# Packing small matmuls into groups of the PE array in an eight-core decoder kernel: gates in row and column groups, pooling bands of 144 columns, sample states in pairs

## The chip, the cores and the metric

The kernel runs on all 8 cores of one Trainium2 chip (two dies: cores 0 to 3 and 4 to 7). Each core computes its own prompt and its own samples. The metric is the device time of the slowest core, in microseconds (us); it is 1 to 2 us longer than the longest span in the trace of the same execution. Some executions fall in a slower state in which one die runs at a lower granted clock (the share of the full TensorE clock that the throttle lets through); only fast executions are compared here. Because the slowest of eight counts, I often give two numbers: the time of the slowest core, and the mean of the spans of all eight cores in the same fast executions. The second is usually less noisy. In the profiles PE is the matmul engine (TensorE), DVE VectorE, ACT ScalarE, POOL GpSimd and SP SyncE; a PSUM bank is one of the buffers into which the PE writes.

## The reference

One layer of a hybrid decoder. Only the parts that the change touches are kept:

```python
D_MODEL, SEQ, DEC_SEQ = 1024, 2048, 4      # per core: one prompt of 2048 rows, 16 samples of 4 rows
GLA_HEADS, GLA_DK, GLA_DV, GLA_GATE_RANK = 4, 128, 256, 16

def token_mix(xn, s0, buf, pos0, p):
    q, k, v, gz, og, u, ga, gb = jnp.split(xn @ p['w_in'], split_points(), axis=-1)     # gz: 16 columns
    log_a = log_sigmoid(gz @ p['w_gk_up'] + p['b_gk']) / 16                             # decay logits
    o, s_new = gla_chunked(q, k, v, log_a, s0)     # S = exp(b_end) * S + k_dec^T v   per head (128 x 256)
    ...

def pool_mix(u, buf, pos0, w_mix, scale):          # trailing means over windows 2, 4, 8, 16 by channel group
    win = hi - cs_shifted_by_w
    d = win / cnt - u
    y = einsum('btgc,gcd->btgd', d, w_mix) * scale
```

After that come a cross-attention over 256 memory tokens and a channel mixer of 4096 hidden units. They make up most of the time and are not changed.

## The kernel before

The kernel declares operations with their reads, their writes and an estimated cost. A list scheduler of its own then fixes one order per engine, from a model of the costs. The engines run their orders strictly one after the other. A DMA is tied to the PE operation that lies `ahead` = 30 us of *declared* PE cost before it, and PSUM banks are given out in the modelled order.

```python
def op(self, eng, fn, reads=(), writes=(), cost=0.1, dma=False, ..., ahead=None, after=()):
    if eng == "pe":
        self.peclk += cost                       # clock of declared PE cost
        self.pelog.append((self.peclk, i))
    ...
    if ahead is not None:                        # a DMA may start once this PE operation is done
        k = bisect.bisect_right(self.pelog, (self.peclk - ahead, 1 << 60)) - 1
        if k >= 0:
            deps[self.pelog[k][1]] = 0
```

Low-rank gate input and decay logits of a tile of 1024 rows (there are two tiles). The output has 16 rows in the first and the contraction is 16 deep in the second, so most of the 128 x 128 array is empty:

```python
def gzp():
    for hf in range(2):
        b = self.bank()
        self.mm(self.pb[b][:16, :], [(self.wgz[:, kc, :], A[:, kc, hf * 512:(hf + 1) * 512]) for kc in range(8)])
        self.cp("act", self.gzT[:, hf * 512:(hf + 1) * 512], self.pb[b][:16, :])
def decay():
    for h in range(4):
        for hf in range(2):
            b = self.bank()
            self.mm(self.pb[b][:, :], [(self.wgk[:, h * 128:(h + 1) * 128], self.gzT[:, hf * 512:(hf + 1) * 512])])
            self.act(T1[:, h, ...], self.pb[b][:, :], AF.Exp, scale=-1.0, bias=self.ncols[:, h:h + 1])
        ...
```

Sample states. The 64 sample rows (16 samples of 4) are the partitions of `kdts` and `vts`. A mask column keeps one sample's 4 rows, so that a 128-deep matmul gives that sample's outer product. Each state (512 KB in fp32) is loaded, copied to bf16, updated in place and stored:

```python
for i in range(SB):                              # SB = 16
    sf = self.ring("s0f", self.s0f); sb_ = self.ring("s0b", self.s0b); kb = self.ring("kblk", self.kblk)
    self.dma("sp", sf[...], I["sgla"][i], nb=1.4)
    self.cp("act", sb_[:, :, :], sf[:, :, :])
    self.ts("dve", kb[:, :], self.kdts[:, :], self.bmk[:, i:i + 1], ALU.mult, also=[sf[:, :, :]])
    self.mmx([... old state times q of sample i, 8 matmuls of 4 columns ...])
    for hp in range(2):
        b = self.bank()
        self.mms([(self.pb[b][:, (h % 2) * 256:(h % 2 + 1) * 256],
                   [(kb[:, h * 128:(h + 1) * 128], self.vts[:, h * 256:(h + 1) * 256])]) for h in (2 * hp, 2 * hp + 1)])
        for h in (2 * hp, 2 * hp + 1):
            self.stt("dve", sf[:, h, :], sf[:, h, :], self.eBs[:, h, i:i + 1], self.pb[b][...], ALU.mult, ALU.add)
        if hp == 0:
            yield                                # other work may come in between
    self.dma("sp", O["sgs"][i], sf[...], nb=1.4)
    yield
```

The 1 MB load of the pooling mix weights, declared without a word about the loads of x:

```python
def precompute(self):
    self.dma("sp", self.pmf[:, :], I["wpmT"][:, :])
```

## Time and profile before

The median of the first six runs was 1296.51 us (1294.37 to 1332.79). The page of the slowest core (core 4) says first how busy each engine was, and the third line gives the engines' shares of the chain of work that ended last.

```profile
span 1293.1 us, 23059 instructions; the slowest of 8 cores (1283.4 to 1293.1 us)
...
PE 1251.0 (97%) x8342; PEld 645.2 (50%) x8490; DVE 654.8 (51%) x1088; ACT 651.4 (50%) x1333; POOL 67.8 (5%) x131
...
PE 91%; DMA 5%; issue 2%; DVE 1%; ACT 1%; DVEq 0%; POOL 0%; ACTq 0%; SPq 0%; POOLq 0%
```

The PE does nearly everything that counts: 97% busy and 91% of the chain. The table of two stretches of core 4 shows where it is not busy. Its first line names the columns.

```profile
core 4: us, PE busy (x) PEld busy (x) DVE busy (x) ACT busy (x) POOL busy (x), PEclk, DMA share, GB/s
0.00:40.00 40.00, 24.59 (x316) 17.12 (x319) 14.27 (x23) 15.80 (x37) 5.37 (x14) 0.81 0.90 197
...
350.00:400.00 50.00, 49.69 (x353) 27.00 (x359) 30.49 (x72) 41.60 (x88) 0.53 (x1) 1.00 0.47 134
```

In the first 40 us the PE works for 24.6 us and the DMA engines are 90% busy: this is the load of x and of the first weights. From 350 to 400 us, where the sample states run, the PE is hardly ever free.

The next lines are from the timeline of core 4 (start, length, engine, line, output and inputs, shape, count, and in brackets the idle time before with what ended it). Ends of matmuls are modelled, so one reads the distance from one start to the next.

```profile
23.25 1.01 PE L842 MATMUL pb<-ident,xn_101 128*128 128x128 bf16 x8 [4.25 <-DVE xn_101 L877]
...
38.57 1.01 PE L842 MATMUL pb<-ident,xn_102 128*128 128x128 bf16 x8 [3.74 <-DVE xn_102 L877]
...
46.69 1.89 PE L814 MATMUL pb<-actT,wgz 128*16 128x512 bf16 x8
...
343.45 1.06 ACT L861 ACTIVATE s0b_140<-s0f_119 128x1024 bf16<-128x1024 f32 x1 [1.05 <-DMA s0f_119<-sgla]
...
371.69 0.34 PE L833 MATMUL pb<-qs,s0b_140 128*128 128x4 bf16 x8
371.90 0.38 PE L824 MATMUL pb<-vts,kblk_142 128*128 128x256 bf16 x2
372.12 0.61 PE L842 MATMUL pb<-ident,xn_102 128*128 128x128 bf16 x8
...
684.15 3.62 PE L814 MATMUL pb<-actT,wgz 128*16 128x512 bf16 x16
```

The two waits at the top are for normalised rows of x, and so for their loads. One group of 16 gate matmuls takes 3.46 us (16 pitches of 216 ns). Two outer products of one sample, a "visit" to the states, take 0.22 us, from 371.90 to 372.12. Last, the issues of the sync engine's DMA queue on the same core: the fourth and the last load of x, then the mix weights.

```profile
17.09 0.33 SPq L915 DMA_DIRECT2D xst_90<-xp  x1
...
26.52 0.33 SPq L915 DMA_DIRECT2D xst_94<-xp  x1
...
31.00 0.33 SPq L915 DMA_DIRECT2D pmf<-wpmT  x1
```

### The profile page before, as it was taken

What the parts mean: (1) busy time and instruction counts of PE and PEld (TensorE: products, weight loads), DVE (VectorE), ACT (ScalarE), POOL (GpSimd) and SP (SyncE); (2) the same over time, 40 slices, a digit from 0 to 9 for tenths busy, and PEclk for the clock granted to TensorE, in tenths of its full rate; (3) what the DMA queues carried; (4) which work ended last, traced back from release to release, by engine and by line L of the source; (5) the groups of instructions that cost most, each with busy time, mean ns of one, the idle gap of its engine ahead of it and who ended that gap; (6) DMA issues with size and microseconds to landing.
All of it is one profiled execution on the core that took longest, in us unless ns stands there. A gap on an engine that the chain in (4) does not pass through costs nothing.

```text
span 1293.1 us, 23059 instructions; the slowest of 8 cores (1283.4 to 1293.1 us)
## 1 busy us (share of the span) xinstructions
PE 1251.0 (97%) x8342; PEld 645.2 (50%) x8490; DVE 654.8 (51%) x1088; ACT 651.4 (50%) x1333; POOL 67.8 (5%) x131
## 2 busy tenths in 40 slices
PE   6899999999999999999999999999999999999997
PEld 4444556444455544444544455644455544454453
DVE  3564755231458765444675356623244754444446
ACT  3555966556587742132236278755558753120304
POOL 1100000000000000000000010100100000000000
PEclk7999999999999999999999999999999999999999
DMA  8979369243829569686779585858862333342503
GB/s 180 187 161 180 70 129 188 42 99 75 219 91 222 138 167 169 113 155 137 154 171 191 93 150 109 147 102 145 142 185 38 62 66 66 66 77 54 98 2 139
DMA packets 33675, 160.93 MB, mean 124 GB/s; under 512 B 4598, under 2 KB 5246, under 8 KB 22156
## 3 DMA queue, kind: packets, MB, share of 16 engines
q0 software_dynamic: 18112, 104.29, 47.9%
q1 hardware_dynamic: 15452, 55.15, 12.3%
q8 instruction: 70, 1.15, 0.4%
q14 instruction: 41, 0.34, 0.1%
HBM read 241.63 MB, written 22.80 MB: 204 GB/s over the span
## 4 chain that ended last, share of the span: by engine, by line
PE 91%; DMA 5%; issue 2%; DVE 1%; ACT 1%; DVEq 0%; POOL 0%; ACTq 0%; SPq 0%; POOLq 0%
PE pb L814 81%; PE pb L824 6%; PE pb L842 3%; DMA wt_45<-wu 1%; PE pb L833 1%; DMA xst_93<-xp 1%; DMA s0f_121<-sgla 1%; DMA xst_89<-xp 1%; DMA sgs<-s0f_121 0%; DMA xst_91<-xp 0%; DVE S L882 0%; DVE xn_102 L882 0%; ACT xn_102 L861 0%; DVE xh L882 0%; DVE xn_101 L882 0%
## 5 line engine op out<-in xcount | busy, mean ns | idle before, releaser
L882 DVE SCALAR_TENSOR_TENSOR xh<-pb,r_178,xh 128x512 f32<-128x512 f32 x128 | 95.7, 750 | 90.8 <-PE pb L814 90.6
L814 PE MATMUL pb<-actT,wt_45 128*128 128x512 bf16 x436 | 100.5, 379 | 0.7
L814 PE MATMUL pb<-actT,wt_44 128*128 128x512 bf16 x435 | 99.1, 379 | 0.7
L861 ACT ACTIVATE tmp_98<-pb 128x512 f32<-128x512 f32 (+1 forms) x48 | 28.4, 591 | 111.7 <-PE pb L814 109.3
L814 PE MATMUL pb<-actT,wt_43 128*128 128x512 bf16 x313 | 71.8, 379 | 0.4
L814 PE MATMUL pb<-actT,wtG 128*128 128x512 bf16 x309 | 71.6, 379 | 0.6
L814 PEld LDWEIGHTS pb<-actT,wt_45 128*128 128x128 bf16 x448 | 43.0, 98 | 50.5 <-issue 0.4
L871 DVE TENSOR_TENSOR xh<-pb,xh 128x512 f32<-128x512 f32 x64 | 44.2, 690 | 47.4 <-PE pb L814 47.1
L814 PEld LDWEIGHTS pb<-actT,wt_44 128*128 128x128 bf16 x448 | 43.2, 98 | 49.7
L861 ACT ACTIVATE tmp_95<-pb 128x512 f32<-128x512 f32 (+1 forms) x49 | 28.5, 581 | 75.2 <-PE pb L814 60.9
L814 PE MATMUL pb<-wt_45,actT 128*128 128x512 bf16 x247 | 57.7, 379 | 1.5 <-DVE xn_101 L882 0.6
L861 ACT ACTIVATE tmp_96<-pb 128x512 f32<-128x512 f32 (+1 forms) x47 | 27.3, 581 | 62.5 <-PE pb L814 61.0
L814 PE MATMUL pb<-actT,wt_46 128*128 128x512 bf16 x247 | 57.4, 379 | 0.5
L814 PE MATMUL pb<-WqK,actT 128*128 128x512 bf16 x247 | 57.4, 379 | 0.5
L861 ACT ACTIVATE tmp_99<-pb 128x512 f32<-128x512 f32 (+1 forms) x48 | 28.3, 590 | 54.2 <-PE pb L814 40.9
L861 ACT ACTIVATE tmp_97<-pb 128x512 f32<-128x512 f32 (+1 forms) x46 | 26.9, 586 | 56.4 <-PE pb L814 45.2
L814 PEld LDWEIGHTS pb<-actT,wtG 128*128 128x128 bf16 x320 | 31.0, 98 | 36.3
L814 PE MATMUL pb<-wt_43,actT 128*128 128x512 bf16 x183 | 45.9, 396 | 3.0 <-DVE actT L871 2.6
L814 PEld LDWEIGHTS pb<-actT,wt_43 128*128 128x128 bf16 x320 | 30.7, 98 | 35.5 <-issue 0.2
L814 PE MATMUL pb<-o2T,wt_44 128*128 128x512 bf16 x192 | 45.0, 379 | 0.0
L871 DVE TENSOR_TENSOR actT<-pb,cols 128x1024 bf16<-128x1024 bf16 x32 | 38.9, 1220 | 11.8 <-PE pb L842 11.4
L814 PE MATMUL pb<-wt_44,actT 128*128 128x512 bf16 x186 | 43.3, 384 | 0.6 <-issue 0.4
(559 smaller groups left out, 2366.3 us busy)
## 6 DMA issues: line engine op xcount, KB each, us to landing
wt_44<-wu POOLq DMA_DIRECT2D x19, 1024.0 KB, 9.9
wt_43<-wu POOLq DMA_DIRECT2D x17, 1024.0 KB, 10.6
wt_45<-wu POOLq DMA_DIRECT2D x17, 1024.0 KB, 12.1
wt_46<-wu POOLq DMA_DIRECT2D x16, 1024.0 KB, 11.2
wtG<-wu POOLq DMA_DIRECT2D x13, 1024.0 KB, 11.8
xh<-xp SPq DMA_DIRECT2D x16, 512.0 KB
yp<-xh SPq DMA_DIRECT2D x15, 512.0 KB, 4.9
wt_46<-wscratch SPq DMA_DIRECT2D x2, 1024.0 KB, 16.6
```

Source lines behind the costliest of these rows:

```text
L814: ins = e.matmul(out, l, r, start=(start and i == 0), stop=(stop and i == m - 1))
L824: ins = e.matmul(out, l, r, start=(i == 0), stop=(i == m - 1))
L833: ins = e.matmul(o, l, r, start=s, stop=t, skip_group_check=True)
L842: ins = e.transpose(o, i, d)
L861: return self.g.op("act", lambda e: e.activation(out=out, in_=in_, func=func, scale=scale, **kw), reads=rd, writes=wr, cost=c)
L871: return self.g.op(eng, lambda e: e.tensor_tensor(out=out, in0=in0, in1=in1, op=op), reads=[in0, in1], writes=[out], cost=self.vcost(eng, ...
L882: return self.g.op(eng, lambda e: e.scalar_tensor_tensor(out=out, in0=in0, scalar=scalar, in1=in1, op0=op0, op1=op1), reads=rd, writes=[ou ...
```

## The change

Four families of small matmuls are made to fill the array. (1) The gate input is computed for four blocks of 256 rows at a time, in four column groups of 32. (2) The decay logits use four row groups, with the weights repeated four times. (3) The pooling bands become 144 columns wide, so that one matmul writes its own block and the 16 rows that reach into the next one: five matmuls to a bank instead of eight. (4) The states are handled two samples at a time (i and i+8). Their rows lie in different groups of 32 partitions, so one masked copy serves both, and the two outer products use two row groups at once. Each writes a bank of its own. The declared costs of the packed groups are divided by `par`.

```diff
-            for hf in range(2):
-                b = self.bank()
-                self.mm(self.pb[b][:16, :], [(self.wgz[:, kc, :], A[:, kc, hf * 512:(hf + 1) * 512]) for kc in range(8)])
-                self.cp("act", self.gzT[:, hf * 512:(hf + 1) * 512], self.pb[b][:16, :])
+            b = self.bank()
+            self.mmx([(self.pb[b][32 * j:32 * j + 32, :256], self.wgz[:, kc, :], A[:, kc, j * 256:(j + 1) * 256], kc == 0, kc == 7)
+                      for kc in range(8) for j in range(4)], par=3.0)
+            self.cp("act", self.gzT[:, :], self.pb[b][:, :256])
 ... decay(): the same idea, for two heads at once ...
+                    bs = [self.bank() for _ in range(4)]
+                    self.mms([(self.pb[bs[j]][:, x * 256:(x + 1) * 256],
+                               [(self.wgk[32 * j:32 * j + 32, (h + x) * 128:(h + x + 1) * 128], self.gzT[32 * j:32 * j + 32, :])])
+                              for x in range(2) for j in range(4)], par=2.5)
 ... pooling ...
-                        items += [(o, l, self.pm01[:, 0, g, :], True, False),
-                                  (self.pb[b][:, s4 * 128:s4 * 128 + 16], self.ur[:, pr, csl], self.pm01[:, 1, g, :16], False, True)]
+                        n = 144 if s4 < 3 else 128
+                        items.append((self.pb[b][:, o:o + n], l, self.pmx[:, g, :n]))
 ... states ...
-        for i in range(SB):
+        for i in range(SB // 2):
+            pair = (i, i + 8)
+            sf = [self.ring("s0f", self.s0f) for _ in pair]
+            kb = self.ring("kblk", self.kblk)
+            self.ts("dve", kb[:, :], self.kdts[:, :], self.bmk[:, i:i + 1], ALU.mult, also=[f[:, :, :] for f in sf])
+            for k, n in enumerate(pair):
+                self.dma("sp", sf[k][...], I["sgla"][n], nb=1.4)
+            for k, n in enumerate(pair):
+                ... copy to bf16, old state times q, as before ...
+            yield
             for hp in range(2):
-                b = self.bank()
+                bs = [self.bank() for _ in pair]
+                self.mms([(self.pb[bs[k]][:, (h % 2) * 256:(h % 2 + 1) * 256],
+                           [(kb[32 * k:32 * k + 32, h * 128:(h + 1) * 128], self.vts[32 * k:32 * k + 32, h * 256:(h + 1) * 256])])
+                          for h in hs for k in range(2)], par=1.8)
+                ... four updates on DVE; both stores after the second half ...
```

More of the change, by code (lines that the diff above doesn't have):

```diff
@@ L466, in make_consts @@
         pm[:, 0, g], pm[:, 1, g], pm[:, 2, g], pm[:, 3, g] = cur, prev, hi, lo
-    c["pm01"] = np.ascontiguousarray(pm[:, 0:2])
+    c["pmx"] = np.ascontiguousarray(np.concatenate([pm[:, 0], pm[:, 1, :, :16]], axis=2))
     c["pm23"] = np.ascontiguousarray(pm[:, 2:4])
@@ L487, in make_consts @@
     c["smu"] = mu
-    bk = np.zeros((128, SB), np.float32)
+    bk = np.zeros((128, SB // 2), np.float32)
     for b in range(SB):
-        bk[b * ST:(b + 1) * ST, b] = 1.0
+        bk[b * ST:(b + 1) * ST, b % 8] = 1.0
     c["bmk"] = bk
@@ L565, in __init__ @@
         inp("ckT", [SB, 128, 2048]); inp("cv", [SB, 128, 2048])
-        inp("wu", [NU, 128, 4096]); inp("wgz", [128, 128]); inp("wgk", [16, 512]); inp("wpmT", [128, 2048])
+        inp("wu", [NU, 128, 4096]); inp("wgz", [128, 256]); inp("wgk", [128, 512]); inp("wpmT", [128, 2048])
         inp("cols", [128, NCOL]); inp("g_fin", [D])
@@ L663, in alloc @@
         self.junk = g.sb("junk", J, [128, 1024], BF16)
-        self.gzT = g.sb("gzT", J, [16, 1024], BF16)
+        self.gzT = g.sb("gzT", J, [128, 256], BF16)
         G = reg(8192)
@@ L720, in alloc @@
         self.rst64 = small("rst64", [128, 256], BF16)
-        self.pm01 = small("pm01", [128, 2, 4, 128], BF16)
+        self.pmx = small("pmx", [128, 4, 144], BF16)
         self.smb = small("smb", [120, 2, 4, 64], BF16)
         self.smu = small("smu", [128, 4, 64], BF16)
-        self.bmk = small("bmk", [128, SB], F32)
+        self.bmk = small("bmk", [128, SB // 2], F32)
         self.cols = small("cols", [128, NCOL], F32)
         self.ncols = small("ncols", [128, 12], F32)
-        self.wgz = small("wgz", [128, 8, 16], BF16)
-        self.wgk = small("wgk", [16, 512], BF16)
+        self.wgz = small("wgz", [128, 8, 32], BF16)
+        self.wgk = small("wgk", [128, 512], BF16)
         self.gzs = small("gzs", [16, 64], BF16)
@@ L816, in mm, with mms @@
         return self.g.op("pe", fn, reads=[x for p in pairs for x in p], writes=[out], cost=len(pairs) * self.mcost(out))
-    def mms(self, groups):
+    def mms(self, groups, par=1.0):
         def fn(e):
@@ L826, in mms, with mmx @@
         c = sum(len(p) * self.mcost(o) for o, p in groups)
-        return self.g.op("pe", fn, reads=[x for o, p in groups for q in p for x in q], writes=[o for o, p in groups], cost=c)
-    def mmx(self, items):
+        return self.g.op("pe", fn, reads=[x for o, p in groups for q in p for x in q], writes=[o for o, p in groups], cost=c / par)
+    def mmx(self, items, par=1.0):
         def fn(e):
@@ L835, in mmx @@
         c = sum(self.mcost(x[0]) for x in items)
-        return self.g.op("pe", fn, reads=[y for x in items for y in x[1:3]], writes=[x[0] for x in items], cost=c)
+        return self.g.op("pe", fn, reads=[y for x in items for y in x[1:3]], writes=[x[0] for x in items], cost=c / par)
     def trs(self, items):
@@ L971, in consts3 @@
         d("pool", self.maskT[:], I["c_maskT"][:, :])
-        d("pool", self.pm01[:], I["c_pm01"][:, :, :, :])
+        d("pool", self.pmx[:], I["c_pmx"][:, :, :])
         d("pool", self.pm23[:], I["c_pm23"][:, :, :, :])
@@ L1076, in decay @@
             for h in range(4):
-                for hf in range(2):
-                    b = self.bank()
-                    self.mm(self.pb[b][:, :], [(self.wgk[:, h * 128:(h + 1) * 128], self.gzT[:, hf * 512:(hf + 1) * 512])])
-                    self.act(T1[:, h, hf * 512:(hf + 1) * 512], self.pb[b][:, :], AF.Exp, scale=-1.0, bias=self.ncols[:, h:h + 1])
+                if h % 2 == 0:
+                    bs = [self.bank() for _ in range(4)]
+                    self.mms([(self.pb[bs[j]][:, x * 256:(x + 1) * 256],
+                               [(self.wgk[32 * j:32 * j + 32, (h + x) * 128:(h + x + 1) * 128], self.gzT[32 * j:32 * j + 32, :])])
+                              for x in range(2) for j in range(4)], par=2.5)
+                for j, b in enumerate(bs):
+                    self.act(T1[:, h, j * 256:(j + 1) * 256], self.pb[b][:, (h % 2) * 256:(h % 2 + 1) * 256], AF.Exp, scale=-1.0,
+                             bias=self.ncols[:, h:h + 1])
                 self.act(T1[:, h, :], T1[:, h, :], AF.Ln, bias=self.ncols[:, 5:6])
@@ L1235, in tile @@
                 b = self.bank()
+                pr = (self.ublk(ti, hf * 4) + 8) % 9
                 items = []
+                if not (first and hf == 0):
+                    items.append((self.pb[b][:, :16], self.ur[:, pr, csl], self.pmx[:, g, 128:]))
                 for s4 in range(4):
-                    s = hf * 4 + s4
-                    cu = self.ublk(ti, s)
-                    pr = (cu + 8) % 9
-                    o = self.pb[b][:, s4 * 128:(s4 + 1) * 128]
-                    l = self.ur[:, cu, csl]
-                    if first and s == 0:
-                        items += [(o, l, self.pm23[:, 0, g, :], True, False), (o, l, self.pm23[:, 1, g, :], False, True)]
-                    else:
-                        items += [(o, l, self.pm01[:, 0, g, :], True, False),
-                                  (self.pb[b][:, s4 * 128:s4 * 128 + 16], self.ur[:, pr, csl], self.pm01[:, 1, g, :16], False, True)]
+                    o = s4 * 128
+                    l = self.ur[:, self.ublk(ti, hf * 4 + s4), csl]
+                    if first and hf == 0 and s4 == 0:
+                        items += [(self.pb[b][:, :128], l, self.pm23[:, 0, g, :]), (self.pb[b][:, :128], l, self.pm23[:, 1, g, :]),
+                                  (self.pb[b][:, 128:144], l, self.pmx[:, g, 128:])]
+                    else:
+                        n = 144 if s4 < 3 else 128
+                        items.append((self.pb[b][:, o:o + n], l, self.pmx[:, g, :n]))
+                items = [x + (i == 0, i == len(items) - 1) for i, x in enumerate(items)]
                 self.mmx(items)
@@ L1590, in gz @@
                 b = self.bank()
-                self.mm(self.pb[b][:16, :64], [(self.wgz[:, kc, :], X[:, kc, :]) for kc in range(8)])
+                self.mm(self.pb[b][:16, :64], [(self.wgz[:, kc, :16], X[:, kc, :]) for kc in range(8)])
                 self.cp("act", self.gzs[:, :], self.pb[b][:16, :64])
                 b = self.bank()
-                self.mms([(self.pb[b][:, h * 64:(h + 1) * 64], [(self.wgk[:, h * 128:(h + 1) * 128], self.gzs[:, :])]) for h in range(4)])
+                self.mms([(self.pb[b][:, h * 64:(h + 1) * 64], [(self.wgk[:16, h * 128:(h + 1) * 128], self.gzs[:, :])]) for h in range(4)])
                 for h in range(4):
@@ L1699, in states @@
                   for j in range(8)])
-        for i in range(SB):
-            sf = self.ring("s0f", self.s0f)
-            sb_ = self.ring("s0b", self.s0b)
+        for i in range(SB // 2):
+            pair = (i, i + 8)
+            sf = [self.ring("s0f", self.s0f) for _ in pair]
             kb = self.ring("kblk", self.kblk)
-            self.dma("sp", sf[:, :, :].rearrange("p h v -> p (h v)"), I["sgla"][i], nb=1.4)
-            self.cp("act", sb_[:, :, :], sf[:, :, :])
-            self.ts("dve", kb[:, :], self.kdts[:, :], self.bmk[:, i:i + 1], ALU.mult, also=[sf[:, :, :]])
-            self.mmx([(self.pb[ob][:, j * 64 + i * ST:j * 64 + (i + 1) * ST], sb_[:, j // 2, (j % 2) * 128:(j % 2 + 1) * 128],
-                       self.qs[:, j // 2, i * ST:(i + 1) * ST], False, i == SB - 1 and j == 7) for j in range(8)])
-            for hp in range(2):
-                b = self.bank()
-                self.mms([(self.pb[b][:, (h % 2) * 256:(h % 2 + 1) * 256],
-                           [(kb[:, h * 128:(h + 1) * 128], self.vts[:, h * 256:(h + 1) * 256])]) for h in (2 * hp, 2 * hp + 1)])
-                for h in (2 * hp, 2 * hp + 1):
-                    self.stt("dve", sf[:, h, :], sf[:, h, :], self.eBs[:, h, i:i + 1], self.pb[b][:, (h % 2) * 256:(h % 2 + 1) * 256],
-                             ALU.mult, ALU.add)
-                if hp == 0:
-                    yield
-            self.dma("sp", O["sgs"][i], sf[:, :, :].rearrange("p h v -> p (h v)"), nb=1.4)
@@ new lines, in states @@
+            self.ts("dve", kb[:, :], self.kdts[:, :], self.bmk[:, i:i + 1], ALU.mult, also=[f[:, :, :] for f in sf])
+            for k, n in enumerate(pair):
+                self.dma("sp", sf[k][:, :, :].rearrange("p h v -> p (h v)"), I["sgla"][n], nb=1.4)
+            for k, n in enumerate(pair):
+                sb_ = self.ring("s0b", self.s0b)
+                self.cp("act", sb_[:, :, :], sf[k][:, :, :])
+                self.mmx([(self.pb[ob][:, j * 64 + n * ST:j * 64 + (n + 1) * ST], sb_[:, j // 2, (j % 2) * 128:(j % 2 + 1) * 128],
+                           self.qs[:, j // 2, n * ST:(n + 1) * ST], False, n == SB - 1 and j == 7) for j in range(8)])
@@ new lines, in states @@
+            yield
+            for hp in range(2):
+                bs = [self.bank() for _ in pair]
+                hs = (2 * hp, 2 * hp + 1)
+                self.mms([(self.pb[bs[k]][:, (h % 2) * 256:(h % 2 + 1) * 256],
+                           [(kb[32 * k:32 * k + 32, h * 128:(h + 1) * 128], self.vts[32 * k:32 * k + 32, h * 256:(h + 1) * 256])])
+                          for h in hs for k in range(2)], par=1.8)
+                for h in hs:
+                    for k, n in enumerate(pair):
+                        self.stt("dve", sf[k][:, h, :], sf[k][:, h, :], self.eBs[:, h, n:n + 1],
+                                 self.pb[bs[k]][:, (h % 2) * 256:(h % 2 + 1) * 256], ALU.mult, ALU.add)
+                    if hp == 0:
+                        yield
@@ L1719, in states @@
+            for k, n in enumerate(pair):
+                self.dma("sp", O["sgs"][n], sf[k][:, :, :].rearrange("p h v -> p (h v)"), nb=1.4)
             yield
@@ L1835, in make_in_maps @@
         "wu": wu.reshape(NU, 128, 4096),
-        "wgz": f(w["w_in"][:, 2048:2064].reshape(8, 128, 16).transpose(1, 0, 2).reshape(128, 128)),
-        "wgk": f(p["w_gk_up"][0]), "wpmT": f(wpmT.reshape(128, 2048)),
+        "wgz": f(np.pad(w["w_in"][:, 2048:2064].reshape(8, 128, 16).transpose(1, 0, 2), ((0, 0), (0, 0), (0, 16))).reshape(128, 256)),
+        "wgk": f(np.pad(np.broadcast_to(p["w_gk_up"][0], (4, 16, 512)), ((0, 0), (0, 16), (0, 0))).reshape(128, 512)), "wpmT": f(wpmT.reshape(128, 2048)),
         "cols": _cols_table(p), "g_fin": f(p["norm_final_g"]),
```

## The prediction

> **What bounds it now.** The page of the slowest core gives PE 1251.0 of 1293.1 us busy (97%); PE is 91% of the chain that ended last. A 512-column matmul starts every 216 ns (timeline), clock 0.99. In the table of stretches most idle lies in the first 40 us (PE 24.6 us busy, DMA share 0.90: waiting for rows of x, then weights); from 227 to 684 us PE lacks about 2 us. So PE time removed after 40 us counts fully; a delay of the first loads counts too.
>
> **PE time removed (timeline pitches):**
> - Low-rank gate input: 16 matmuls of 512 columns per tile of 1024 rows = 3.46 us. After: 32 of 256 columns on four column groups. The Trainium skill, "TensorE: Matmul & The Clock Gate", Part 3, measured 2.38x for three column groups and 3.07x for four row groups; about 3x (estimate) leaves 1.15. Saves 2.3, twice: 4.6.
> - Decay logits: 8 x 216 ns = 1.73 us per tile to about 0.65. Saves 1.1, twice: 2.2.
> - Pooling: a 128- plus 16-column pair takes 81 ns (16 matmuls in 0.68 us), four per bank = 324 ns. After: 25 + 3x62 + 56 = 268 ns. 32 banks: 1.8. Fewer instructions may shorten the stall without visible releaser in the first tile's pooling (2.25 us on core 4, then half clock; 0.9 on others): 0.5.
> - Sample states: 64 matmuls x 109 ns = 7.0 us, paired 3.5. But "TensorEngine Tiling (Array Packing)", Key Properties, says a mode change drains; the timeline shows about 0.1 us extra at each entry and exit of the 16-row and 64-column groups. 16 visits x 2 x 0.1 = 3.2. Net 0.3.
>
> Sum: about 9.4 us.
>
> **What it adds.**
> 1. The instruction order moves the 1 MB load of pooling mix weights from behind all x loads to ahead of the fourth; it waits there for the first projection group, which ended near 19 us before. Loads were saturated (197 GB/s in 0 to 40 us), so 1 MB is about 5 us (estimate). The rows landing at 36.0 and 38.7 us, which PE awaited for 3.7 us, come 4 to 5 later. The replicated gate weights (256 KB read, not 32) add up to 1. Part is hidden: cost 4 us.
> 2. Paired states hold two PSUM banks per half for four DVE updates of 474 ns instead of one for two, while DVE is 60 to 80% and ACT 80% busy (350 to 450 us). PE, nearly never idle there, should wait for banks or probabilities: 3 us.
>
> ACT does 16 short exponentials instead of 8 per tile, about 1 us more, off the path.
>
> **Net:** -9.4 + 7 = about -2.5; some added waits may not appear. I say 1292.5 us, 8 in 10 within 1284 to 1301. Faster by over 2%: 0.02; within 2%: 0.96; slower: 0.02.
>
> **Right or wrong shows in:** the first gate group at 48 to 51 us rather than 46.7 on core 4, with PE idle before x transposes grown by about 4 us; gate group about 1.2 us for 32 matmuls; 8 decay matmuls in about 0.35; pooling bank 0.27; state groups of four still about 0.4 including drains; new PE waits of 2 to 5 us between 350 and 500 us for DVE or ACT.
>
> **What would make it wrong:** drains hidden (states save 3 us more); groups not concurrent (4 us lost); the early 1 MB load costing nothing, or more; unexplained stalls appearing elsewhere among dense small instructions.

## The result, and the profile after

The changed kernel ran in 1301.78 us (median of 10 runs; 1295.63 to 1464.6, slow runs included). The kernel before, over 20 runs, had 1296.17. The ratio is 1.0037, with a 95% interval of 1.0024 to 1.0051. A ratio is the mean time of one kernel's fast runs over that of the other's fast runs of the same rounds, so it is not quite the ratio of the medians. The kernel is therefore within 2%, but slower by 0.4% where I expected it faster by 0.3%. (The number that I named, 1292.5 us, lies 4.0 us under the 1296.5 of the first runs, while my sum had given only 2.5.)

The same lines of the page, now for core 0, the slowest:

```profile
span 1299.1 us, 23081 instructions; the slowest of 8 cores (1284.8 to 1299.1 us)
...
PE 1253.4 (96%) x8450; PEld 636.4 (49%) x8450; DVE 652.3 (50%) x1080; ACT 651.6 (50%) x1347; POOL 67.7 (5%) x131
...
PE 88%; DMA 5%; ACT 2%; issue 2%; DVE 2%; SPq 0%; DVEq 0%; ACTq 0%; POOLq 0%
```

The PE's share of the chain fell from 91 to 88%; ACT and DVE took most of it over. The two busy times, 1251.0 and 1253.4 us, are of different cores and can't be compared: on core 4 the PE's busy time fell from 1251.0 to 1242.7 us, and on the mean of the eight cores from 1256.5 to 1250.0.

The table of the stretches, core 0, for the time in which the sample states run:

```profile
350.00:400.00 50.00, 48.20 (x369) 24.97 (x370) 28.54 (x61) 39.48 (x82) 0.53 (x1) 1.00 0.39 119
```

Where the PE was busy for 49.7 of 50 us before (core 4), it is now busy for 48.2.

The timeline of the PE, core 0:

```profile
44.69 1.01 PE L842 MATMUL pb<-ident,xn_100 128*128 128x128 bf16 x8 [5.66 <-DVE xn_100 L877]
...
60.52 1.06 PE L833 MATMUL pb<-actT,wgz 128*32 128x256 bf16 x32
61.50 1.91 PE L814 MATMUL pb<-wt_43,acs 128*64 128x512 bf16 x8
63.35 0.40 PE L824 MATMUL pb<-gzT,wgk 32*128 32x256 bf16 x8
63.68 3.63 PE L814 MATMUL pb<-wt_44,actT 128*128 128x512 bf16 x16
...
219.96 0.43 PE L833 MATMUL pb<-pmx,ur 128*128 128x16 bf16 x5
220.23 0.59 PE L814 MATMUL pb<-wt_44,VT 128*128 128x512 bf16 x2
...
393.28 0.39 PE L824 MATMUL pb<-vts,kblk_141 32*128 32x256 bf16 x4
393.60 1.90 PE L814 MATMUL pb<-WqK,actT 128*128 128x512 bf16 x8
```

From start to start: the gate group of 32 takes 0.98 us (before 3.46), eight decay matmuls 0.33 us (two such groups per tile, 0.66; before 8 x 216 ns = 1.73), a pooling bank of five 0.27 us, and four paired outer products with their change of array shape 0.32 us (before, two visits of 0.22 us). Every packed group does what it was meant to do. The Trainium skill, "TensorE: Matmul & The Clock Gate", Part 3, gives 2.38 times for three column groups and 3.07 times for four row groups. Here four column groups gained 3.5 times, and the row groups of the decay logits 2.6 times, with entry and exit included.

So the gain is there, and something else costs more than it. Two things can be seen in the trace. The first is in the issues of the sync engine's queue on core 0: the 1 MB load now stands ahead of the fourth load of x, and the last load of x is issued 5.3 us later than before on core 4 (5.7 us later on core 4 itself, at 32.24).

```profile
19.35 0.33 SPq L915 DMA_DIRECT2D pmf<-wpmT  x1
19.77 0.38 SPq L915 DMA_DIRECT2D xst_90<-xp  x1
...
31.80 0.33 SPq L915 DMA_DIRECT2D xst_94<-xp  x1
```

The second is in the waits. The view of the PE's waits between 330 and 530 us lists nothing at all on cores 0 and 4 of the kernel before. For the changed kernel, core 0, it has these lines (us in total, times, longest):

```profile
PE pb L814 <- DVE mT L871: 2.9, 1, 2.9
PE pb L814 <- DMA wt_43<-wu: 1.7, 1, 1.7
PE pb L824 <- DVE mTs L871: 1.6, 1, 1.6
PE pb L814 <- ACT PT_75 L861: 0.8, 1, 0.8
PE pb L814 <- DMA wtG<-wu: 0.6, 1, 0.6
PE pb L814 <- DVE s0f_119 L882: 0.5, 1, 0.5
PE pb L833 <- ACT s0b_139 L861: 0.3, 1, 0.3
```

That is 8.4 us of new waits in the stretch in which the paired states run. The timeline of all engines of core 0 shows where the larger ones come from:

```profile
345.07 1.06 ACT L861 ACTIVATE s0b_140<-s0f_119 128x1024 bf16<-128x1024 f32 x1 [5.60 <-DMA s0f_119<-sgla]
...
351.28 1.89 PE L814 MATMUL pb<-wt_45,mT 128*128 128x512 bf16 x8 [2.88 <-DVE mT L871]
...
517.26 0.53 POOL L915 DMA_DIRECT2D wtG<-wu  x1 [9.85 <-DMA sgs<-s0f_120]
```

ACT stood idle for 5.60 us for a state that had not landed. Behind the copy of that state in its fixed order are the sigmoid steps which `mT` needs, so the PE waited 2.88 us for `mT`. Before, the same copy stood later in ACT's order, and ACT waited 1.05 us for it. At 517 us the gpsimd engine, which issues the weight loads, had been held for 9.85 us by the store of a state whose buffer shares memory with `wtG`, and the PE's wait of 0.6 us for `wtG` follows. Such a hold is not new: in the kernel before it lasted 11.48 us, but the store was issued at 484.5 us (in the changed kernel at 503.9) and `wtG` was loaded from 491.9, well before its use at 509.3. The starts of the two cores differ by some us, so not all of the 19 us is the pairing. The wait of 1.7 us for `wt_43` has another way: that load was issued at 506.89, before the hold ended. The first down projection now begins with `wt_43`, and in the kernel before it began with `wtG` and needed `wt_43` only at 523.1. So the weight buffers are used in another order; that the late store of the pairs made the scheduler choose it is likely, but not shown. The wait of 1.6 us for `mTs` is one of order too: the last step of the samples' merge (two DVE operations of 0.41 and 0.42 us) now stands between two sample groups which the PE's order puts one right after the other (514.82 and 517.52 us). In the kernel before, the last write of `mTs` was at 533.5 us and its first reader at 551.4.

I divided the kernel into seven stages by landmarks on the PE and averaged the eight cores of one profiled execution of each kernel (us; stages D and E hold all of the visits to the states; "waits" is PE idle time in C to F; the wait for the first matmul on `mT` lengthens C):

| stage | before | after | early load only (e2) | pairs only (e5) | gates and pooling, load late (e4) |
|---|---|---|---|---|---|
| A start, projections, until the first transpose of kd | 129.3 | 128.2 | 134.3 | 130.3 | 125.8 |
| B until the first matmul on smb | 87.9 | 87.6 | 87.9 | 87.9 | 87.6 |
| C until first matmul on mT | 126.0 | 127.2 | 126.6 | 130.9 | 124.6 |
| D output projection | 34.8 | 34.4 | 34.8 | 34.8 | 34.8 |
| E attention, until first down projection | 127.2 | 134.4 | 127.8 | 134.0 | 127.3 |
| F until the last gate matmul of tile 1 | 177.7 | 175.0 | 177.8 | 177.9 | 175.2 |
| G the rest | 605.6 | 605.0 | 606.5 | 605.5 | 603.4 |
| waits in C to F | 0.8 | 7.8 | 1.7 | 10.5 | 0.1 |

Stage E of the changed kernel is 7.2 us longer. About 2.2 us of that is sample work which moved ahead of the landmark; 3.4 us are waits, and the remaining 1.6 us are not accounted for.

### The profile page after: what moved, and what is told of

Read it like the earlier page. It is cut to its first block, busy times and chain, and to the rows that moved or that the text cites. A ratio compares the mean times of both kernels' runs of the same rounds, so it can differ in the third digit from the quotient of the medians.

```text
span 1299.1 us, 23081 instructions; the slowest of 8 cores (1284.8 to 1299.1 us)
## 1 busy us (share of the span) xinstructions
PE 1253.4 (96%) x8450; PEld 636.4 (49%) x8450; DVE 652.3 (50%) x1080; ACT 651.6 (50%) x1347; POOL 67.7 (5%) x131
## 4 chain that ended last, share of the span: by engine, by line
PE 88%; DMA 5%; ACT 2%; issue 2%; DVE 2%; SPq 0%; DVEq 0%; ACTq 0%; POOLq 0%
PE pb L814 79%; PE pb L824 5%; PE pb L842 3%; DMA s0f_119<-sgla 1%; DMA xst_93<-xp 1%; DMA sgs<-s0f_120 1%; PE pb L833 1%; DMA wtG<-wu 1%; DMA xst_91<-xp 1%; ACT tmp_96 L861 0%; ACT xn_100 L861 0%; DVE S L882 0%; DVE xn_102 L882 0%; ACT xn_102 L861 0%; ACT tmp_97 L861 0%
## 5 line engine op out<-in xcount | busy, mean ns | idle before, releaser
L814 PE MATMUL pb<-actT,wt_45 128*128 128x512 bf16 x448 | 101.6, 379 | 0.0
L814 PE MATMUL pb<-actT,wt_44 128*128 128x512 bf16 x448 | 100.3, 379 | 0.0
L814 PE MATMUL pb<-actT,wt_43 128*128 128x512 bf16 x320 | 72.5, 379 | 0.0
L814 PE MATMUL pb<-wt_45,actT 128*128 128x512 bf16 x256 | 59.5, 379 | 0.6 <-DVE xn_101 L882 0.4
L814 PE MATMUL pb<-actT,wt_46 128*128 128x512 bf16 x256 | 58.5, 379 | 0.0
L814 PE MATMUL pb<-wt_43,actT 128*128 128x512 bf16 x192 | 49.8, 407 | 2.3 <-DVE actT L871 2.2
L814 PE MATMUL pb<-wt_43,hid_79 128*128 128x512 bf16 x192 | 44.4, 390 | 1.7 <-DMA wt_43<-wu 1.7
## 6 DMA issues: line engine op xcount, KB each, us to landing
wt_44<-wu POOLq DMA_DIRECT2D x19, 1024.0 KB, 10.4
wt_43<-wu POOLq DMA_DIRECT2D x17, 1024.0 KB, 11.3
```

Of the source, the lines that this page charges most:

```text
L814: ins = e.matmul(out, l, r, start=(start and i == 0), stop=(stop and i == m - 1))
```

## The experiments

Theory: the packed groups pay as predicted, and the paired states cost far more than my 3 us, by their waits; the early load costs about 4 us. Rivals: the change of array shape in the states, not the pairing, is what costs; the early load is the whole loss; or the packed gates do not save in place what their pitches say. All kernels below gave correct outputs. Each was timed in five rounds.

### e1: the changed kernel with the mix weights behind the sixth load of x

```diff
-        self.dma("sp", self.pmf[:, :], I["wpmT"][:, :])
+        self.dma("sp", self.pmf[:, :], I["wpmT"][:, :], after=self.xld[5:6])
```

> The changed kernel, with only the 1 MB load of the pooling mix weights put back behind the eight loads of x (it now waits for the sixth of them to land). Theory (the early load costs the start): about 4 us less than the changed kernel, so about 1 us over the kernel before, ratio to before 1.000 to 1.002; the fourth x load is issued near 17 us and not 19.8, the last x is transposed some 4 us earlier; nothing changes between 350 and 520 us. Rival (the loss is all in the paired states or in the array's shape changes): no gain, ratio 1.003 to 1.005.

Measured: 1.0033 (1.0014 to 1.0052), median 1303.07 us. Its fast runs average 1301.0 us, against 1296.6 for the kernel before. Putting the load back did not bring the kernel below the one before. The early load is not the whole loss.

### e2: the kernel before with the mix weights ahead of x

```diff
-        self.dma("sp", self.pmf[:, :], I["wpmT"][:, :])
+        self.dma("sp", self.pmf[:, :], I["wpmT"][:, :], ahead=34.0)
```

> The kernel before, with only that 1 MB load put ahead of the fourth x load, nothing else. Theory: 3 to 5 us slower than before, ratio 1.002 to 1.004, all of it before the first gate group; matmul groups unchanged. Rival (its place costs nothing because the loads are needed anyway by 70 us): ratio 0.999 to 1.001.

Measured: 1.0038 (1.0023 to 1.0053), median 1302.58 us. The issues of the sync engine on core 0 show that the edit did what it should, with the load ahead of the last five loads of x:

```profile
19.90 0.33 SPq L915 DMA_DIRECT2D pmf<-wpmT  x1
20.32 12.92 SPq L915 DMA_DIRECT2D xst<-xp  x5
```

Stage A grew by 5.0 us and nothing else by more than 1. Alone, the early load costs 5.0 us on the slowest core and 3.1 us on the mean of the cores.

### e3: the changed kernel with the old states

```diff
-        for i in range(SB // 2):
-            pair = (i, i + 8)
-            ... paired block and its mask of 8 columns ...
+        for i in range(SB):
+            ... block and mask of 16 columns of the kernel before ...
```

> The changed kernel with the sample states put back to one at a time over all 128 rows; gates, pooling and the early 1 MB load stay. Theory (pairing brings waits of 6 to 9 us between 340 and 525 us: the ACT queue held by a state load ahead of gate work, PE waiting for banks, late weight loads behind the state stores): about 7 us less than the changed kernel, ratio to before about 0.998 (0.996 to 1.000), and the waits on mT and mTs and on weights near 520 us are gone. Rival (all of the loss is at the start): as the changed kernel, ratio 1.003 to 1.005.

Measured: 0.9961 (0.9944 to 0.9979), median 1291.31 us. Without the pairs the changed kernel beats the kernel before by 5.7 us (8.0 on the mean of the cores), even with the early load. The view of the PE's waits from 330 to 530 us is empty again (core 4).

### e4: both undone

```diff
 e3, and
-        self.dma("sp", self.pmf[:, :], I["wpmT"][:, :])
+        self.dma("sp", self.pmf[:, :], I["wpmT"][:, :], after=self.xld[5:6])
```

> Both undone: gates and pooling of the change, states one at a time, the 1 MB load behind x. Theory: the whole saved PE time stays, 9 us (gates 2 x 2.5 and decay 2 x 1.2, pooling 1.8) off before: ratio 0.992 to 0.995, about 1287 us, faster than both kernels. Rival (gates and pooling gain nothing on the path, or their gain is eaten by array shape changes): ratio 0.998 to 1.001.

Measured: 0.9915 (0.9902 to 0.9927), median 1286.25 us. Packed gates, decay and pooling together save 11.0 us on the slowest core and 10.9 on the mean of the cores. Against e1, which differs by the pairs alone and ran on the same chip, it is 15.3 us faster (12.3 on the mean).

### e5: the kernel before with paired states only

```diff
-        for i in range(SB):
+        for i in range(SB // 2):
+            pair = (i, i + 8)
+            ... paired block and mask of the changed kernel, with par=1.8 ...
```

> The kernel before with the paired states alone (row groups included); gates, pooling and the place of the 1 MB load as before. Theory (pairing costs by the waits it brings, about 9 us between 330 and 530 us and a little after, against 0.7 us saved on the array): 6 to 11 us slower than before, ratio 1.005 to 1.009; the stretch from the first scores of the cross attention to the first down projection 7 us longer, as in the changed kernel. Rival (the paired outer products do save 3 us, and it was the combination with the early load that hurt): ratio 0.997 to 1.000.

I compare fast runs. The kernel before had 1296.67 and 1293.72 us; e5 had 1307.29 to 1309.6 us in four runs. The pairs alone cost about 13 us on the slowest core, and 11.3 on the mean of the cores. The view of the PE's waits, core 3, 330 to 530 us, names the same waits as in the changed kernel:

```profile
PE pb L814 <- DVE mT L871: 3.7, 1, 3.7
PE pb L824 <- DVE mTs L871: 1.6, 1, 1.6
PE pb L814 <- DMA wt<-wu: 1.2, 1, 1.2
...
```

With three smaller ones (`PT` 0.7, `s0f` 0.5, `s0b` 0.3) this is 8.0 us, with no packed gate and no early load in the kernel: these waits belong to the pairs. On the mean of the eight cores the waits in C to F grew by 9.7 us, most of the 11.3.

### e6: pairs without row groups

```diff
-                           [(kb[32 * k:32 * k + 32, h * 128:(h + 1) * 128], self.vts[32 * k:32 * k + 32, h * 256:(h + 1) * 256])])
+                           [(kb[k][:, h * 128:(h + 1) * 128], self.vts[:, h * 256:(h + 1) * 256])])
 (a mask and a masked copy for each sample again, and no par=1.8; everything else of the changed kernel kept)
```

> The changed kernel with the paired order kept (loads, stores, two banks per half), but each outer product over all 128 rows with its own mask, so without row groups and without changes of array shape. Theory (the order of the pairs costs, not the array): like the changed kernel or up to 3 us slower, since nothing runs side by side and DVE makes twice as many masks: ratio to before 1.003 to 1.007. Rival (row groups and shape changes cost): as fast as the changed kernel with the old states, ratio 0.995 to 0.998.

Measured: only two fast runs, 1301.42 and 1310.01 us. The size cannot be read from this. Neither run comes near the 1290 us or so which would follow if the row groups, and not the pairing, were what costs. It is inconclusive as to size and speaks against that rival. The profile says: cores 4 to 7 were not slowed (clock 0.984 to 0.994), and there the waits are back without any row group (for `mT` 2.4 and 2.2 us, for `mTs` 1.6, on cores 4 and 7). Stage E took 135.5 to 147.4 us on these four cores, against 127.1 to 127.4 in the kernel before. So the waits don't need the change of array shape. On cores 4 and 7 one wait of 6.0 us for a state copy comes on top, which the changed kernel has not, so the length is not a measure of the pairs.

### e7: row groups without pairs

```diff
-                           [(kb[:, h * 128:(h + 1) * 128], self.vts[:, h * 256:(h + 1) * 256])]) for h in (2 * hp, 2 * hp + 1)])
+                           [(kb[i // 8 * 32:i // 8 * 32 + 32, h * 128:(h + 1) * 128],
+                             self.vts[i // 8 * 32:i // 8 * 32 + 32, h * 256:(h + 1) * 256])]) for h in (2 * hp, 2 * hp + 1)])
 (the kernel before; one sample at a time, so nothing runs side by side)
```

> The kernel before with one edit: each outer product reads only the 32 rows of its half (row group 0 or 1) instead of 128 rows with zeros; one sample at a time, so nothing runs side by side. It measures the shape changes by themselves. A visit of four paired matmuls took 0.39 us in the changed kernel, of which 0.22 are columns, so a visit costs 0.17 us more than its columns. Theory: 32 visits cost about 5 us on PE and nothing is given back, no new waits: ratio 1.003 to 1.005. Rival (shape changes are hidden): ratio 0.999 to 1.001.

Measured: four fast runs of 1299.65 to 1300.43 us, about 5 us over the two fast runs of the kernel before. The PE's timeline on core 4 (this core was not slowed in the profiled execution) shows what it is:

```profile
364.37 0.34 PE L833 MATMUL pb<-qs,s0b 128*128 128x4 bf16 x8
364.65 0.39 PE L824 MATMUL pb<-vts,kblk 32*128 32x256 bf16 x2
364.97 0.62 PE L842 MATMUL pb<-ident,xn 128*128 128x128 bf16 x8
```

From 364.37 to 364.97 is 0.60 us. Before, the same three starts (371.69 to 372.12) span 0.43 us. One visit in another array shape costs 0.17 us more, before it and after it together. The kernel has 32 such visits: 32 x 0.17 = 5.4 us, and the runs show about 5. The stages show the same without leaning on two runs: D and E together take 167.3 us on the mean of the eight cores, against 162.0 before, all at a clock of 1.00, and waits there are 0.2 us. (Outside the states, stops without a releaser in the first tile's pooling, of up to 2.5 us, were longer than before in this execution.) So the shape change by itself costs PE time and no waits among the states. With pairs there are 16 visits (2.7 us), and the two outer products side by side about pay for it: 0.32 us for a paired visit against 2 x 0.22 us, with 0.07 us more before it. The shape change is real but is not the loss.

### e8: gates only

```diff
 e4, and the pooling loop of the kernel before (bands of 128 and 16 columns)
```

> As the version that undid states and load order (ratio 0.9915), but with the old pooling too: only the gate and decay groups are changed. Theory: it loses the 1.8 us of the wide bands, and up to 2 us more if the stall in the first pooling comes back: ratio 0.993 to 0.9955. Rival (the wide bands give nothing): 0.991 to 0.992.

Measured: five fast runs of 1285.21 to 1288.54 us (mean 1286.83), about 8 us under the two fast runs of the kernel before. Most of e4's gain is the gates and the decay logits. The pooling is worth what is left, 1 to 3.5 us, which these runs do not separate well (they also stand on different chips).

### e11 and e12: the changed kernel and e1 again, on one chip

> The changed kernel again, unchanged, to stand on the same chip as the next three. Ratio to before 1.0024 to 1.0051 as at first.

> The changed kernel with only the 1 MB load back behind x, a second time, because the first (1.0033) gave back nothing while the same edit gave 5 us on the version with the old states. If the costs simply add: 4 to 5 us less than the changed kernel in this call. If the pairs swallow it (their later waits differ from core to core and run to run, and the slowest core decides): within 2 us of the changed kernel again.

Measured: e11, the changed kernel unedited, 1.0040 (1.0017 to 1.0063). On the mean of the cores it is 2.4 us over the kernel before (1292.12 against 1289.71); on the slowest core it is 4.9. e12, with the edit of e1, 1.0016 (0.9993 to 1.0038), 2.6 us faster than e11, with intervals that overlap. In the kernel with pairs the early load is worth 0 to 3 us, less than the 5 us it costs without them (e2; and e3 over e4). Why it is partly swallowed there was not settled.

### e9: the changed kernel with the first state copies later in ACT's order

```diff
-                self.cp("act", sb_[:, :, :], sf[k][:, :, :])
+                self.g.op("act", ... the same copy ..., reads=[sf[k][:, :, :]] + ([self.mT[:, 7, 512:]] if i == 0 else []), ...)
 (the first pair's copies also declare that they read the last part of mT, so they come after it)
```

> The changed kernel with one edit: the first two copies of sample states on ACT come after the last write of the merged branch output, so that ACT no longer sits before a state load while gate sigmoids stand behind it. Theory: the wait of PE on the merged output (1.7 us mean of eight cores, up to 2.9) goes, the other waits of the pairs stay: 1 to 3 us less than the changed kernel of this call. Rival (ACT was not the cause): the wait stays, no change.

Measured: 1.0039 (1.0010 to 1.0068), beside 1.0040 of e11. In the PE's waits from 330 to 530 us (core 0) the wait for `mT` is gone, and the others stand; these are the longest:

```profile
PE pb L814 <- DMA wt<-wu: 1.8, 1, 1.8
PE pb L824 <- DVE mTs L871: 1.6, 1, 1.6
...
```

Four more follow, of 0.5 to 1.1 us, and none of them is for `mT`.

The wait for `mT` fell from 2.0 us (e11) to 0 on the mean of the cores. The mean span of the cores fell by 2.0 us (1292.12 to 1290.09), and the time of the slowest core did not move; with intervals of 0.3% a gain of 2 us there is not excluded. The order on ACT is the cause of that wait, and the wait is a small part of the whole.

### e10: what the findings suggest

```diff
 e4, and
-        d("pool", self.wgk[:], I["wgk"][:, :])
+        d("pool", self.wgk[:], I["wgk"][:, :], after=x)
 (the same for the two reset tables rst512 and rst64: all three wait for the sixth load of x)
```

> The version that beat both (gates and pooling of the change, old states, 1 MB load behind x: ratio 0.9915), with the widened gate weights and two small constant tables also issued after the sixth x load has landed and no longer at 2.7 us. Theory (start is bound by loads; 256 KB + 384 KB read in front of x are up to 3 us of traffic, an estimate from 197 GB/s): 1 to 3 us faster: ratio 0.9895 to 0.991. Rival (they fit in gaps, or the gates now wait for their weights): 0.991 to 0.993.

Measured: 0.9903 (0.9889 to 0.9917), median 1282.52 us (1281.58 to 1284.75). It beats both kernels: packed gates, decay and pooling, the states as they were, and the large and the small loads behind the sixth load of x. Whether the last step adds to e4 (0.9915) is likely (1 to 2 us) but not separated by these intervals.

### A loss that stays open

In the second tile's pooling the PE stands still on some cores for 2 to 4 us without any releaser in the record. The PE's timeline of the changed kernel, core 4:

```profile
831.34 0.37 PE L833 MATMUL pb<-pmx,ur 128*128 128x16 bf16 x4
835.59 1.77 PE L833 MATMUL pb<-pmx,ur 128*128 128x128 bf16 x16 [3.87 <-issue]
```

The table of stretches of the same core shows a granted clock (third number from the right) of 0.75 in the 10 us after the stall; in the next 10 us it was 1.00:

```profile
836.00:846.00 10.00, 9.78 (x65) 5.43 (x64) 2.65 (x4) 4.88 (x8) 0.53 (x1) 0.75 1.01 152
```

The Trainium skill, "TensorE: Matmul & The Clock Gate", Part 1, says that the clock drops to half after an idle window of about 3.4 us. The trace agrees in kind: in steps of 2 us the clock is 0.50 from 836 to 840 us, then 0.77, then 1.00. But a stop of 2.25 us (core 4 of the kernel before, until 222.12 us) was followed by 0.50 as well, from 222.6 to 226.0, so here a shorter stop was enough. So a stall of this kind costs its length, and about 2.5 us again (10 us at 0.75, an estimate). It appeared in the profiled fast execution of every kernel that has both the pairs and the wide bands: stalls of 2.2 us or more on three cores of the changed kernel, and on two to four cores of e1, e9, e11 and e12. (e6 has both too and showed none, but its profile is of a slow execution.) In all other kernels the longest such stall between 805 and 880 us was 1.3 us (e8, just behind the pooling), and e3, e4 and e10 had none. Whether it explains why the slowest core lost 4.9 us where the mean lost 2.4 is not shown: in the profiled execution the slowest core, core 0, had no such stop. DMA engines were also about 80 to 100% busy from 824 to 838 us in kernels without the stop (e3, e4, e8, e10), so this alone does not explain it. I have no experiment that takes it away by itself.

The traces do hold a strong hint. The page lists a DMA queue of the kind "instruction" (packets, MB, share of 16 engines):

```profile
q8 instruction: 69, 1.13, 0.3%
```

Its packets have 16 KB and come once in about 19 us, one for each 257 PE instructions (matmuls, weight loads and others) that core 4 recorded. On core 4 of the changed kernel one of them landed at 834.28 us, and the PE went on at 835.59. In the 14 traces, all 57 PE stops of 0.8 us or more which have no releaser (after the first 60 us) end 0.7 to 1.8 us after the landing of a q8 packet; by chance about 6% would. So in these stops the PE most likely waited for its own instructions. That is a coincidence in time found in every case, not an experiment, and it leaves open why the pairs together with the wide bands make the stops in the second tile long.

## Why the prediction was right or wrong

The time, 1301.78 us as the median of all ten runs, is just above the predicted range of 1284 to 1301; the median of the fast runs, 1300.9, is just inside it. Within 2% was right, but the direction was wrong: my sum gave 2.5 us less, and it was about 5 us more. That the time came so near the range is partly luck: a gain larger than predicted hid part of a loss that was far larger. The ledger, from differences of fast means (us on the slowest core / on the mean of the cores):

| term | predicted | measured |
|---|---|---|
| gates, decay, pooling | -9.1 | -11.0 / -10.9 (e4 over before) |
| early load of mix weights | +4 | +5.3 / +2.9 (e3 over e4) |
| paired states (drains, work, waits) | +2.7 | +10.6 / +10.4 (e11 over e3, each against the kernel before; e1 over e4, e12 over e4 and e5 over before give 13.0 to 15.3 / 11.3 to 12.3) |
| sum | -2.4 | +4.9 / +2.4 |

The measured rows are steps from the kernel before over e4 and e3 to e11, so they add up by construction, and another order of steps would share the loss out differently.

Point by point:

- "PE time removed after 40 us counts fully": right. e4 gained a little more than the pitches promised.
- Sizes of the packed groups: gate group "about 1.2 us", measured 0.98; eight decay matmuls "about 0.35", measured 0.33; pooling bank "0.27", measured 0.27; state groups of four "about 0.4 including drains", measured 0.39 (0.32 from start to start, and 0.07 before it).
- Drains, "16 visits x 2 x 0.1 = 3.2": e7 measured 0.17 a visit, so 2.7 us. The Trainium skill, "TensorEngine Tiling (Array Packing)", Key Properties, says that a mode switch drains the array; the trace agrees in so far as a visit in another shape costs 0.17 us more.
- The early load, "cost 4 us": right in mechanism and near in size without the pairs (5.3 / 2.9); in the kernel with pairs, taking it away gave only 0 to 3 us. PE idle before the transposes of x was to grow by about 4 us on core 4. It did not grow there (8.0 to 6.8 us), but it did on core 0 (4.2 to 12.5), and from 6.5 to 9.3 on the mean of the cores: 2.8 us. All of the idle time of stage A rose by 2.1 us on the mean (13.6 to 15.7). The first gate group came at 52.5 us on core 4, and not at "48 to 51". This sign was a poor one: the new order also puts more projection groups ahead of the group, and in e4, without the early load, it stands at 53.6 us on core 4.
- **The step that failed:** "Paired states hold two PSUM banks per half ... PE ... should wait for banks or probabilities: 3 us". The term is mis-sized by more than three times, and its mechanism was only the smaller part. Waits of the predicted kind are 0.8 (`PT`), 0.5 (bank) and 0.3 us (state copy), 1.6 us in all on core 0. The other 6.8 us of the 8.4 came by ways that I had not followed: a state copy ahead of the sigmoid steps in ACT's fixed order (2.9), weights (1.7 with the buffers in another order, 0.6 behind a store that frees shared memory late), and the samples' merge step `mTs` (1.6), which now directly follows the group that it depends on. On the mean of the eight cores the waits in C to F grew by 7.0 us, against a loss of 10.4 on the mean; the rest I can't assign in full. I costed what one visit of a pair does to the PE, and not what holding two of four state buffers at once does to the order of loads, copies and stores. Only the copy's place was tried alone (e9). The pairs' two buffers, their order of loads and their places for other work (`yield`) were always changed together, so which of them makes the other waits is not separated.
- "PE, nearly never idle there": right (49.7 of 50 us), and the likely reason why the waits cost so much: there was no slack to hide a late input.
- "Fewer instructions may shorten the stall ... 0.5": half right. Stops without a releaser in the first tile's pooling fell from 0.68 to 0.47 us on the mean of the cores, in one execution of each (before: 2.25 us on core 4, 0.9 to 1.4 on three others, none on four), but stalls of up to 3.87 us appeared in the second tile. "Unexplained stalls appearing elsewhere among dense small instructions" was on my list of what could make the prediction wrong. This one did appear; the traces point to the loads of PE instructions, but no experiment shows it.

## What to carry to other kernels

Packing small matmuls into row and column groups pays what the pitches say, as long as the visit is long enough to repay about 0.17 us for the change of array shape, and as long as nothing else has to be regrouped for it. When packing needs two items in flight where there was one, cost the ring of buffers, the in-order engine that prepares the items, and whatever shares their memory, before the matmuls: here 0.8 us of PE time was to be won (16 x 0.05 us, from the pitches) and more than 10 us were lost (of these, 7 to 10 us are waits in the traces). After any edit under a scheduler, compare the order of the DMA issues too, because a smaller declared cost can move an unrelated load.

## What the Trainium skill lacked or had wrong

- "TensorEngine Tiling (Array Packing)", Key Properties, says that switching the tiling mode drains the array but gives no size. Here a visit to 32-row groups between full-array matmuls cost 0.17 us (e7: 0.60 against 0.43 us), about 5 us for 32 visits.
- "TensorE: Matmul & The Clock Gate", Part 3, has speed-ups for three column groups (2.38), for four row groups (3.07) and for both kinds together. It has none for four column groups alone or for short groups with entry and exit: here 3.5 times (3.46 to 0.98 us), and 2.6 times for row groups of eight matmuls.
- The same page, Part 1, tells one to expect a clock of 13/16 for sustained dense matmuls on all cores. In the fast executions here the means of the cores were 0.983 to 0.995. Only slow executions had the lower clock on a whole die: in one of e2's, cores 0 to 3 had 0.83 and spans of over 1510 us, and cores 4 to 7 had 0.99 and 1290 to 1293 us.
- "Runtime: NRT & Kernel Launch", Instruction fetch mechanics, calls the cost of fetching the next block of instructions mostly hidden. Here it seems to show: PE stops of 0.8 to 3.9 us without a releaser, among dense small matmuls, end 0.7 to 1.8 us after a packet of the instruction queue, in all 57 cases (3.87 us on core 4 of the changed kernel).
